# A hybrid encoder in float32: keys projected ahead of queries, the memory's parts ahead of both, and one recurrent block kept on chip

## The chip, the cores and the metric

The kernel runs on one core of a Trainium2 chip. The metric is the device time of one execution in microseconds (us). The core has TensorE (matmuls, PE in the profile; its weight loads are PEld), VectorE (DVE), ScalarE (ACT), GpSimd (POOL, which here mostly issues DMAs) and SyncE (SP, which issues the other DMAs). SBUF is the memory on chip, PSUM the accumulators of TensorE, DRAM the memory off chip.

## The reference

Two layers over 512 positions of width 1024. Each layer projects its input `h` with one large matrix into the inputs of five branches: dilated attention (A), a recurrence run in both directions (B), grouped attention with rotation (C), differential attention (D) and attention to a memory of 256 rows (M). Their gated outputs go through one product each, weighted by a gate that is computed from `h`, and then through an output product and a layer norm.

```python
h = layer_norm(x, ln_in_g, ln_in_b)
for l in range(DEPTH):
    p = jnp.einsum('bsd,dc->bsc', h, w_in[l])
    pa, pb, pc, pd, pm = split_last(p, mixer_sizes)
    o_a = mixer_dilated(pa, table_a)
    o_b = mixer_rwkv(pb, ...)
    o_c = mixer_axial_gqa(pc, ...)
    o_d = mixer_diff(pd, ..., table_d, l)
    o_m = mixer_memory(pm, mem, w_mem_kv[l])
    y = gated_merge(h, (o_a, o_b, o_c, o_d, o_m), w_branch[l], w_gate[l], b_gate[l])
    out = jnp.einsum('bsd,de->bse', y, w_out[l])
    h = layer_norm(alpha * h + out, ln_g[l], ln_b[l])
```

`gated_merge` is the sum over the branches of `sigmoid(h @ w_gate + b_gate) * (o @ w_branch)`. In attention, `o = softmax(q kᵀ / 8 + bias) v`, per head of 64 channels (in D the difference of two such softmaxes).

## The kernel before

**Numbers and products.** Everything is float32. A value that enters a product is split into a high part, rounded to TensorE's faster float32 form, and a low rest: ScalarE casts the high part, VectorE subtracts it. `gemm3_steps` (lines 145 to 152) then makes three matmuls per block of 128 rows. `hT` holds the layer's input this way for the whole layer.

**A projection** (`proj`, lines 161 to 163) makes one block of 128 output channels for all 512 positions: 24 matmuls into a PSUM tile `pg`, of which there are two. Its weights come in two halves of 256 KB: `load_w` loads each into a slot `wraw` (two slots on each of the channels "r" and "f") over SP's queue, `split_w` (lines 129 to 138) casts it on ScalarE to `whi` and subtracts on VectorE to `wlo`, two slots each. So the weights of a following projection are loaded and split while TensorE works on the current one. `proj_halves` makes two projections at once, in two stretches of 256 positions.

**Attention.** For a pair of heads (A, M) or one head of D the program projects the query, then the key, then the value. `q_stack` (lines 420 to 425) brings the query into high and low parts with two ScalarE and two VectorE instructions. `k_stack` (lines 427 to 437) does the same for the key, and then copies each of the four halves to the other 64 partitions by a DMA of 128 KB, issued on POOL's queue. `score` (lines 439 to 443) makes two matmuls for each block of 128 queries, one with `kh`, one with `kl`, into one of two PSUM tiles `psc`. `softmax` (lines 445 to 463) reads them on VectorE and ScalarE, `transposed` turns the result on TensorE, and `pv_head` or `pv` multiplies with the values. The value goes through the copy `vT` on ScalarE and four transposes on TensorE (line 501). `silu2` (lines 347 to 354) makes the gate, which takes one more projection, and `gated` multiplies it in, at the end of a pair or a head. In the first pair of A query and key are projected by `proj_halves`; in the first layer their weights are loaded at the kernel's start (line 285) and split at line 292.

**The memory.** In the first layer's first two pairs `memory_kv` (lines 260 to 266) projects the memory's keys and values for both layers and stores them in `scr_kv` in DRAM. Branch M (lines 681 to 702) loads them with one DMA of 512 KB into a tile `kvm` of a pool that is opened after D's pool is closed, projects the query, and then stacks the key and splits the value.

**Branch products.** The outputs of C, D and M, and of the recurrence's four blocks (pairs of heads, `finish`, lines 1054 to 1086), are stored in `scr_o` in DRAM (`spill`, and lines 1082 and 1085). `branch_steps` (lines 369 to 392) makes a branch's gate and product for eight blocks of channels; `reload` (lines 361 to 367) loads the outputs over POOL's queue into tiles `o`, of which there are four. The products of A, C, D and M are steps of the generator `fl`, from which `pull` takes some during C, M and the recurrence, so that TensorE has work between the steps of a slow chain. The product of the recurrence (line 1134) is made in the last stage of a layer together with the output product, the residual `z` and the layer norm.

**The order.** The program gives no order across engines. The framework plans it when the program is built: what comes earlier in the program has priority, instructions are placed as they become ready and as tile slots come free, and each engine and each DMA queue then works in that fixed order. In the trace, matmuls of a following projection stand between scores, for instance. A pool opened later may use the memory of a closed one only after the last use of its tiles.

Of the kernel before, what the change touches and what calls it, by code (L numbers as in the profile page):

```python
# [9 lines left out]
F32 = mybir.dt.float32  # L10
# [9 lines left out]
S = 512  # L20
# [32 lines left out]
def encoder_kernel(ctx: ExitStack, tc: tile.TileContext, x, mem, ln_in, rel_bias, w_in, par, w_up, a_up,  # L53
# [218 lines left out]
    with tc.tile_pool(name="init", bufs=1) as ip:  # L272
# [11 lines left out]
        load_x(3)  # L284
        raws = [load_w(w_in[0, b], 1024, ch) for b, ch in zip((0, 4), "rf")]
        for t in range(2):
# [37 lines left out]
    for l in range(L):  # L324
# [10 lines left out]
        ot = []  # L335
        y = [None] * 8

        def new_o():
# [29 lines left out]

        def branch_steps(br, os, nk, done=None, ch="f", pool=wp, gb=1):
            k0 = K0[br]  # L370
            if os is None:
                os = reload(br, nk)
            for db in range(8):
                ps = ps_f() if ch == "f" else ps_s()
                w = split_w(w_gate[l, br * 8 + db], 1024, "f")
                yield from gemm3_steps(ps, [(*wk(w, k), hT[:, 0, k, :], hT[:, 1, k, :]) for k in range(8)])
                gt = pool.tile([128, S], F32, name="gt", tag="gt", bufs=gb)
                i = br * 8 + db
                act(gt, ps, AF.Tanh, scale=0.5, bias=hb[:, i:i + 1])
                ps = ps_f() if ch == "f" else ps_g()  # L380
                w = split_w(w_branch[l, db, :, k0 * 128:(k0 + nk) * 128], nk * 128, ch)
                yield from gemm3_steps(ps, [(*wk(w, k), os[k][:, 0, :], os[k][:, 1, :]) for k in range(nk)])
                if y[db] is None:
                    y[db] = big.tile([128, S], F32, name="y", tag="y", bufs=8)
                    stt(y[db], gt, 1.0, ps, ALU.add, ALU.mult)  # L385
                else:
                    stt(gt, gt, 1.0, ps, ALU.add, ALU.mult)  # L387
                    if done is None:
                        tt(y[db], y[db], gt, ALU.add)
                    else:  # L390
                        tt(gt, y[db], gt, ALU.add)
                        done(db, gt)
# [17 lines left out]
        with tc.tile_pool(name=f"att{l}", bufs=1) as at:  # L410
# [115 lines left out]
            for hp in range(4):  # L526
# [5 lines left out]
                if hp == 0:  # L532
                    proj_halves((ps, ps2), l, (0, 4), hT, "rf", ws0 if l == 0 else None)
                else:
                    proj(ps, l, hp, hT)
                    proj(ps2, l, 4 + hp, hT, "f")
                q = q_stack(ps)
                k = k_stack(ps2)
                ps = ps_g()
# [4 lines left out]
                if l == 0 and hp < L:  # L544
                    for b in range(4):
                        memory_kv(hp, b)
                of = tile_of("of", [128, S], F32, 2)
                for i in range(2):
                    b = load_bias(2 * hp + i)
# [6 lines left out]
                    pv_head(of, p4, 4, lambda kb: v[:, i, kb, :], i)  # L556
                g2 = silu2(at, l, 12 + hp, ch="f")
                oA.append(gated(of, g2))
# [69 lines left out]


            with tc.tile_pool(name=f"attd{l}", bufs=1) as ad:  # L630
                lt = ad.tile([128, 4, 64], F32, name="lt", tag="lt")
# [11 lines left out]
                for h in range(4):  # L643
                    ps = ps_g()
                    proj(ps, l, 44 + h, hT)
                    q = q_stack(ps)
                    ps = ps_g()
                    proj(ps, l, 48 + h, hT)
                    k = k_stack(ps)
                    ps = ps_g()  # L650
# [29 lines left out]

            with tc.tile_pool(name=f"attm{l}", bufs=1) as am:
                kv = am.tile([128, 4, 256], F32, name="kvm", tag="kvm")
                nc.sync.dma_start(out=kv, in_=scr_kv[l].rearrange("b p t -> p b t"))
                for b in range(2):
                    ps = ps_g()
                    proj(ps, l, 60 + b, hT)
                    q = q_stack(ps)
                    k = k_stack(kv[:, b, :], 256)
                    v = v_pair(kv[:, 2 + b, :], 2)
                    of = tile_of("of", [128, S], F32, 2)  # L690
                    for i in range(2):
                        p4 = []
                        for qb in range(4):
                            ps = ps_s()
                            score(ps, q, k, i, qb, 256)
                            p, _ = softmax(ps, 256, None, (DVE, ACT)[qb % 2])
                            p4.append(p)
                            pull(0.3)
                        pv_head(of, p4, 2, lambda kb: v[:, i, kb, :], i)
                    g2 = silu2(at, l, 62 + b)  # L700
                    t = gated(of, g2, True)
                    spill(4, b, t)


        with tc.tile_pool(name=f"rw{l}", bufs=1) as rp:
# [6 lines left out]
            def recurrence():  # L712
# [341 lines left out]
                def finish(p):  # L1054
# [23 lines left out]
                    g2 = silu2(rp, l, 16 + 14 + p, 1, "ysq")  # L1078
                    stt(ys, ys, 0.5, g2, ALU.mult, ALU.mult)
                    hi = rp.tile([128, S], F32R, name="yhi", tag="ysq", bufs=1)  # L1080
                    nc.scalar.copy(hi, ys)
# [30 lines left out]
        with tc.tile_pool(name=f"out{l}", bufs=1) as op:  # L1112
# [20 lines left out]
            gb = load_gb(op, lnp[l])  # L1133
            for _ in branch_steps(1, None, 4, done, "r", op, 2):
                pass
# [137 lines left out]
```

## Time and profile before

| | us |
|---|---|
| median of 3 runs | 2314.18 |
| lowest and highest run | 2313.76, 2317.56 |
| profiled execution | 2311.92 |
| its span, first to last instruction | 2310.1 |
| TensorE busy | 2206.5 (96%) |
| VectorE busy | 1733.0 (75%) |
| ScalarE busy | 1273.5 (55%) |
| mean granted TensorE clock | 0.991 of full |

In the profiled execution the first layer's A runs to about 215 us, C to about 345, D to about 490, M to about 530, the recurrence to about 1056 and the layer's last stage to about 1180; the second layer follows with the same stages. The profile is read from TensorE: where a matmul is preceded by idle time, the view of waits names what released it. Times of the timeline count from the first instruction.

### The profile page before, as it was taken

Reading aid. Unit: us, or ns where it says so; the run is one execution under the profiler, and the core shown is the slowest. Engines: PE = TensorE matmul, PEld = TensorE weight load, DVE = VectorE, ACT = ScalarE, POOL = GpSimd, SP = SyncE. Lnnn points to the kernel's source line nnn. Section 1 sums busy time; section 2 is a strip of 40 time slices with the busy share of each in tenths; the row PEclk is TensorE's granted clock in tenths of the full one; section 3 lists DMA queues with packets and bytes.
Section 4 is the critical chain, followed back from the end, with each engine's and each line's share of the span. In section 5 each row is a group of like instructions: output and inputs, shape, how many; then the busy total and the mean of one; then the engine's idle time right before and its main releaser. Section 6 shows DMA issues by size and latency. Waiting matters only on the chain.

```text
span 2310.1 us, 36289 instructions
## 1 busy us (share of the span) xinstructions
PE 2206.5 (96%) x13056; PEld 1690.5 (73%) x13056; DVE 1733.0 (75%) x4236; ACT 1273.5 (55%) x2785; POOL 60.9 (3%) x119
## 2 busy tenths in 40 slices
PE   6999999999999999999999999999999999999998
PEld 5877777777677777776877777777677777777676
DVE  7676886576889797965567778766778979878455
ACT  3555666675655565544235656666675646555440
POOL 0000000000000000000000000000000000000000
PEclk9999999999999999999999999999999999999999
DMA  7733123332222221315334321232312222222350
GB/s 261 230 95 86 64 76 96 105 95 80 73 79 70 93 77 60 108 51 190 101 116 104 94 64 62 94 99 83 114 60 92 74 65 94 72 93 67 100 180 37
DMA packets 112612, 222.58 MB, mean 96 GB/s; under 512 B 13304, under 2 KB 23288, under 8 KB 112048
## 3 DMA queue, kind: packets, MB, share of 16 engines
q1 hardware_dynamic: 102000, 196.14, 26.5%
q0 software_dynamic: 10432, 24.12, 4.1%
q8 instruction: 103, 1.69, 0.3%
q14 instruction: 77, 0.63, 0.1%
HBM read 188.71 MB, written 28.36 MB: 94 GB/s over the span
## 4 chain that ended last, share of the span: by engine, by line
PE 53%; issue 17%; DVE 17%; ACT 7%; DMA 5%; POOL 0%; SPq 0%; DVEq 0%; POOLq 0%; ACTq 0%
PE pg L150 7%; PE pg L151 7%; PE pg L149 7%; PE pf L149 5%; PE pf L150 4%; PE pf L151 4%; PE psc L443 3%; DVE pr L959 2%; DVE W L961 2%; PE po L488 2%; PE pt L469 2%; DVE wlof L136 1%; PE psc L151 1%; PE psc L150 1%; PE psc L149 1%
## 5 line engine op out<-in xcount | busy, mean ns | idle before, releaser
L150 PE MATMUL pg<-hT,whir 128*128 128x512 f32 (+1 forms) x912 | 366.0, 401 | 0.5 <-DVE hT L176 0.5
L149 PE MATMUL pg<-hT,whir 128*128 128x512 f32 (+1 forms) x912 | 364.4, 400 | 1.9 <-DVE q L424 1.6
L151 PE MATMUL pg<-hT,wlor 128*128 128x512 f32 (+1 forms) x912 | 364.3, 399 | 1.7 <-DVE wlor L136 1.7
L136 DVE TENSOR_TENSOR wlor<-wrawr,whir 128x512 fp32r<-128x512 f32 x240 | 163.7, 687 | 123.2 <-ACT whir L135 114.5
L135 ACT CAST whif<-wrawf 128x512 fp32r<-128x512 f32 (+1 forms) x272 | 164.6, 606 | 149.9 <-PE pf L150 87.4
L135 ACT CAST whir<-wrawr 128x512 fp32r<-128x512 f32 x240 | 147.5, 618 | 178.4 <-PE pg L150 111.9
L149 PE MATMUL pf<-hT,whif 128*128 128x512 f32 x512 | 223.0, 435 | 8.9 <-DVE y L385 5.0
L136 DVE TENSOR_TENSOR wlof<-wrawf,whif 128x512 fp32r<-128x512 f32 (+1 forms) x272 | 181.6, 669 | 48.3 <-ACT whif L135 43.1
L150 PE MATMUL pf<-hT,whif 128*128 128x512 f32 x512 | 208.3, 407 | 0.0
L151 PE MATMUL pf<-hT,wlof 128*128 128x512 f32 x512 | 207.7, 406 | 0.0
L151 PEld LDWEIGHTS pg<-hT,wlor 128*128 128x128 f32 x912 | 172.2, 189 | 40.6 <-DVE wlor L136 4.2
L149 PEld LDWEIGHTS pg<-hT,whir 128*128 128x128 f32 x912 | 172.4, 189 | 38.8 <-ACT whir L135 2.6
L150 PEld LDWEIGHTS pg<-hT,whir 128*128 128x128 f32 x912 | 172.2, 189 | 37.8 <-issue 3.6
L176 DVE TENSOR_TENSOR pT<-pt,pT 128x512 fp32r<-128x512 f32 x176 | 114.2, 686 | 36.3 <-ACT pT L175 34.9
L175 ACT CAST pT<-pt 128x512 fp32r<-128x512 f32 x176 | 94.6, 588 | 63.7 <-PE pt L469 62.6
L149 PEld LDWEIGHTS pf<-hT,whif 128*128 128x128 f32 x512 | 97.5, 190 | 41.2 <-DVE gt L387 10.7
L469 PE MATMUL pt<-cst,p 128*128 128x128 f32 x704 | 118.6, 273 | 0.0
L151 PEld LDWEIGHTS pf<-hT,wlof 128*128 128x128 f32 x512 | 97.3, 190 | 22.4 <-issue 1.6
L959 DVE TENSOR_TENSOR pr<-W,U 128x60 f32<-128x60 f32 (+24 forms) x496 | 103.8, 209 | 11.9
L150 PEld LDWEIGHTS pf<-hT,whif 128*128 128x128 f32 x512 | 98.0, 191 | 18.9 <-issue 3.9
L961 DVE TENSOR_TENSOR W<-W,pr 128x60 f32<-128x60 f32 (+24 forms) x496 | 102.8, 207 | 10.8
L469 PEld LDWEIGHTS pt<-cst,p 128*128 128x128 f32 x704 | 89.7, 141 | 27.3 <-DVE p L460 2.9
(324 smaller groups left out, 4836.9 us busy)
## 6 DMA issues: line engine op xcount, KB each, us to landing
wrawr<-in_w_in_dram SPq DMA_DIRECT2D x224, 256.0 KB, 2.8
wrawf<-in_w_gate_dram SPq DMA_DIRECT2D x160, 256.0 KB, 2.8
o<-scr_o POOLq DMA_DIRECT2D x28, 512.0 KB, 4.5
wrawf<-in_w_branch_dram SPq DMA_DIRECT2D x48, 256.0 KB, 2.7
bias<-scr_toe SPq DMA_DIRECT2D x24, 448.0 KB, 3.3
scr_o<-os SPq DMA_DIRECT2D x20, 512.0 KB, 3.1
wrawf<-in_w_in_dram SPq DMA_DIRECT2D x32, 256.0 KB, 3.2
wrawr<-in_w_out_dram SPq DMA_DIRECT2D x32, 256.0 KB, 3.0
```

What stands on the lines that cost most here:

```text
L135: nc.scalar.copy(hi, raw)
L136: tt(lo, raw, f(hi), ALU.subtract)
L149: mm(ps, ah, bh, start=(i == 0), stop=False)
L150: mm(ps, ah, bl, start=False, stop=False)
L151: mm(ps, al, bh, start=False, stop=(i == n - 1))
L175: nc.scalar.copy(hi, src)
L176: tt(lo, src, f(hi), ALU.subtract)
L443: mm(ps[:, :nk], q[:, i, sl], part[:, i if g is None else g, :nk], start=(j == 0), stop=(j == 1))
L469: nc.tensor.transpose(pt[:, qb * 128:(qb + 1) * 128], p4[qb][:, kb * 128:(kb + 1) * 128], ident)
L488: mm(po, vwin(kb), pT[:, b, :], start=(kb == 0 and b == 0), stop=(kb == nkb - 1 and b == 1))
L959: tt(pr, W[:, t8, s:s + 1].to_broadcast([128, nt, n]), U[:, s:s + 1, rsl].to_broadcast([128, nt, n]), ALU.mult)
L961: tt(W[:, t8, rsl], W[:, t8, rsl], pr, ALU.add)
```

## The change

1. In A and D the key is projected and stacked ahead of the query. In the first pair of A, key and query change places in the interleaved projection; the key keeps channel "r" of the two. In the other pairs the key takes channel "r" and the query "f".
2. In the first pair of A the gate's projection (`silu2`) stands ahead of the scores instead of behind the products.
3. The memory's keys and values are loaded ahead of D, into the two tiles `qf` that C used, by two DMAs of 256 KB. In M the key is stacked and the value split ahead of the query's projection.
4. The recurrence's last block (p = 3) is split into a tile `o` and stays on chip: it is neither stored nor reloaded. The branch product of the recurrence starts with this block; `order` keeps weights and blocks together.

```diff
-        raws = [load_w(w_in[0, b], 1024, ch) for b, ch in zip((0, 4), "rf")]
+        raws = [load_w(w_in[0, b], 1024, ch) for b, ch in zip((4, 0), "rf")]
...
+        oB = []
...
-        def branch_steps(br, os, nk, done=None, ch="f", pool=wp, gb=1):
+        def branch_steps(br, os, nk, done=None, ch="f", pool=wp, gb=1, order=None):
...
-                yield from gemm3_steps(ps, [(*wk(w, k), os[k][:, 0, :], os[k][:, 1, :]) for k in range(nk)])
+                yield from gemm3_steps(ps, [(*wk(w, k), o[:, 0, :], o[:, 1, :]) for k, o in zip(order or range(nk), os)])
...
                 if hp == 0:
-                    proj_halves((ps, ps2), l, (0, 4), hT, "rf", ws0 if l == 0 else None)
+                    proj_halves((ps2, ps), l, (4, 0), hT, "rf", ws0 if l == 0 else None)
                 else:
-                    proj(ps, l, hp, hT)
-                    proj(ps2, l, 4 + hp, hT, "f")
+                    proj(ps2, l, 4 + hp, hT)
+                    proj(ps, l, hp, hT, "f")
+                k = k_stack(ps2)
                 q = q_stack(ps)
-                k = k_stack(ps2)
...
                 of = tile_of("of", [128, S], F32, 2)
+                g2 = silu2(at, l, 12 + hp, ch="f") if hp == 0 else None
                 for i in range(2):
...
-                g2 = silu2(at, l, 12 + hp, ch="f")
+                g2 = g2 or silu2(at, l, 12 + hp, ch="f")
...
+            kvm = [tile_of("qf", [128, S], F32, 2).rearrange("p (b t) -> p b t", b=2) for _ in range(2)]
+            for i in range(2):
+                nc.sync.dma_start(out=kvm[i], in_=scr_kv[l, 2 * i:2 * i + 2].rearrange("b p t -> p b t"))
...
                 for h in range(4):
                     ps = ps_g()
+                    proj(ps, l, 48 + h, hT)
+                    k = k_stack(ps)
+                    ps = ps_g()
                     proj(ps, l, 44 + h, hT)
                     q = q_stack(ps)
-                    ps = ps_g()
-                    proj(ps, l, 48 + h, hT)
-                    k = k_stack(ps)
...
-            with tc.tile_pool(name=f"attm{l}", bufs=1) as am:
-                kv = am.tile([128, 4, 256], F32, name="kvm", tag="kvm")
-                nc.sync.dma_start(out=kv, in_=scr_kv[l].rearrange("b p t -> p b t"))
-                for b in range(2):
-                    ps = ps_g()
-                    proj(ps, l, 60 + b, hT)
-                    q = q_stack(ps)
-                    k = k_stack(kv[:, b, :], 256)
-                    v = v_pair(kv[:, 2 + b, :], 2)
...
+            for b in range(2):
+                k = k_stack(kvm[0][:, b, :], 256)
+                v = v_pair(kvm[1][:, b, :], 2)
+                ps = ps_g()
+                proj(ps, l, 60 + b, hT)
+                q = q_stack(ps)
...
                     stt(ys, ys, 0.5, g2, ALU.mult, ALU.mult)
+                    if p == 3:
+                        oB.append(finish_o(rp, ys))
+                        return
                     hi = rp.tile([128, S], F32R, name="yhi", tag="ysq", bufs=1)
...
-            for _ in branch_steps(1, None, 4, done, "r", op, 2):
+            for _ in branch_steps(1, oB + reload(1, 3), 4, done, "r", op, 2, (3, 0, 1, 2)):
```

The rest of branch M is the same text, one level further out.

## Rows read from the trace of the kernel before

**Rows 1.** The page: busy time of each engine, share of the span, instructions.

```profile
PE 2206.5 (96%) x13056; PEld 1690.5 (73%) x13056; DVE 1733.0 (75%) x4236; ACT 1273.5 (55%) x2785; POOL 60.9 (3%) x119
```

**Rows 2.** Whom TensorE waited for, whole span: us in total, times, longest us.

```profile
PE psc L443 <- DMA kl<-kl: 9.0, 9, 3.1
PE pg L149 <- DMA o<-scr_o: 8.4, 2, 5.2
PE psc L443 <- DMA kh<-kh: 6.1, 12, 1.0
PE pt L501 <- DMA kvm<-scr_kv: 1.4, 2, 0.8
```

**Rows 3.** Stretches: length, busy us (instructions) per engine; then TensorE clock, DMA share, GB/s.

```profile
386.78:393.00 6.22, 6.13 (x21) 4.80 (x22) 4.71 (x15) 4.03 (x10) 0.00 (x0) 0.73 0.15 43
1069.29:1075.00 5.71, 5.71 (x18) 4.54 (x19) 2.34 (x4) 2.20 (x5) 0.00 (x0) 0.70 0.82 310
1198.20:1204.00 5.80, 5.80 (x20) 4.64 (x21) 5.37 (x18) 3.65 (x10) 0.00 (x0) 0.71 0.19 57
1512.33:1519.00 6.67, 6.23 (x20) 4.59 (x21) 4.43 (x12) 4.02 (x9) 0.00 (x0) 0.74 0.16 49
2197.56:2205.00 7.44, 7.44 (x22) 5.87 (x23) 3.77 (x6) 2.75 (x5) 0.00 (x0) 0.64 0.30 115
```

**Rows 4.** Whom TensorE waited for in branch D: first layer, then second layer.

```profile
PE psc L443 <- DMA kh<-kh: 2.2, 4, 1.0
PE psc L443 <- DMA kl<-kl: 1.5, 2, 1.2
...
PE psc L443 <- DMA kl<-kl: 3.9, 4, 2.2
PE psc L443 <- DMA kh<-kh: 2.5, 4, 1.0
```

**Rows 5.** One projection of 24 matmuls as a stretch, in the columns of rows 3.

```profile
1189.10:1194.74 5.64, 5.64 (x24) 4.59 (x25) 2.64 (x4) 1.47 (x3) 2.07 (x4) 1.00 0.89 252
```

**Rows 6.** Timeline, one head of D: start, us, engine, instruction, [idle before]; then loads' landing.

```profile
1506.02 0.33 SPq L359 DMA_DIRECT2D scr_o<-os  x1
1508.35 0.51 POOL L436 DMA_DIRECT2D kl<-kl  x1 [0.22 <-issue]
1512.33 0.50 PE L443 MATMUL psc<-kl,q 128*128 128x512 f32 x1 [2.15 <-DMA kl<-kl]
1513.36 0.62 ACT L135 CAST whir<-wrawr 128x512 fp32r<-128x512 f32 x1 [5.39 <-DMA wrawr<-in_w_in_dram]
1514.01 0.59 ACT L653 COPY vT<-pg 128x512 f32<-128x512 f32 x1
...
DMA to landing us min/median/max: 2.7/2.9/5.9
```

**Rows 7.** Timeline, second layer, first head pair of A.

```profile
1198.20 0.47 PE L443 MATMUL psc<-kl,q 128*128 128x512 f32 x1 [3.06 <-DMA kl<-kl]
1198.40 0.29 DVE L635 TENSOR_TENSOR lp<-lt 128x128 f32<-128x128 f32 x1 [5.08 <-DMA lt<-in_d_lambda_dram]
```

**Rows 8.** The first layer: last reader of tile qf, and (timeline) first use of kvm.

```profile
L424 DVE SCALAR_TENSOR_TENSOR q<-qf,q x2: 685/686/687, 306.7 to 307.5; 64x512 fp32r<-64x512 f32 x2
...
495.19 0.41 PE L501 MATMUL pt<-cst,kvm 128*128 128x128 f32 x2 [0.59 <-DMA kvm<-scr_kv]
```

**Rows 9.** Timeline, end of the second layer's recurrence; then its stall as a stretch.

```profile
2184.40 0.68 DVE L1084 TENSOR_TENSOR ys<-ys,yhi 128x512 fp32r<-128x512 f32 x1
2185.11 0.36 SPq L1085 DMA_DIRECT2D scr_o<-ys  x1
2189.34 0.54 POOL L365 DMA_DIRECT2D o<-scr_o  x1 [6.04 <-DMA scr_o<-ys]
2197.56 0.79 PE L149 MATMUL pg<-o,whir 128*128 128x512 f32 x1 [5.18 <-DMA o<-scr_o]
...
2192.00:2197.60 5.60, 0.42 (x3) 0.04 (x1) 0.03 (x1) 0.00 (x0) 0.00 (x0) 0.86 1.04 385
```

More of the change, by code (lines that the diff above doesn't have):

```diff
@@ L678, in encoder_kernel @@
                     spill(3, h, t)
-            with tc.tile_pool(name=f"attm{l}", bufs=1) as am:
-                kv = am.tile([128, 4, 256], F32, name="kvm", tag="kvm")
-                nc.sync.dma_start(out=kv, in_=scr_kv[l].rearrange("b p t -> p b t"))
-                for b in range(2):
-                    ps = ps_g()
-                    proj(ps, l, 60 + b, hT)
-                    q = q_stack(ps)
-                    k = k_stack(kv[:, b, :], 256)
-                    v = v_pair(kv[:, 2 + b, :], 2)
[L690 to L702, printed above, removed]
+            for b in range(2):
[4 more added lines that the diff above has]
+                q = q_stack(ps)
+                of = tile_of("of", [128, S], F32, 2)
+                for i in range(2):
+                    p4 = []
+                    for qb in range(4):
+                        ps = ps_s()
+                        score(ps, q, k, i, qb, 256)
+                        p, _ = softmax(ps, 256, None, (DVE, ACT)[qb % 2])
+                        p4.append(p)
+                        pull(0.3)
+                    pv_head(of, p4, 2, lambda kb: v[:, i, kb, :], i)
+                g2 = silu2(at, l, 62 + b)
+                t = gated(of, g2, True)
+                spill(4, b, t)
         with tc.tile_pool(name=f"rw{l}", bufs=1) as rp:
```

## The prediction

> **What bounds the kernel now.** I read the page's busy times first: TensorE is busy 96% of the span, VectorE 75%, ScalarE 55% [rows 1]. So time comes back only where TensorE stands still and the work behind the stall isn't held by something else at the same moment. The list of who TensorE waited for shows which stalls the change can reach [rows 2]: the score matmuls (line 443) wait for the copies of the key halves, 9.0 us for `kl` and 6.1 us for `kh`; the first branch product after the recurrence waits 8.4 us in two places for the reload of `o` from DRAM; the transposes of the memory's values wait 1.4 us for `kvm`. Together 24.9 us of 2310.1.
>
> Then I read the granted clock in the stretches right behind the five longest of these stalls [rows 3]. It is a mean of stretches at the upper and at the lower level (2.4 and 1.2 GHz): 0.73, 0.70, 0.71, 0.74 and 0.64. TensorE is busy in nearly all of them, so each costs (1 − clock) × its length: 1.7, 1.7, 1.7, 1.7 and 2.7 us, in sum 9.5. A stall of 2 to 5 us is thus followed here by another 1.7 to 2.7 us lost to slow matmuls. The ceiling of the change is 24.9 + 9.5 = 34.4 us.
>
> By stage: the differential branch (D) has waits of 2.2 + 1.5 us in the first layer and 3.9 + 2.5 in the second [rows 4], 10.1, and two of the slow stretches (behind 386.78 and 1512.33), 13.5 together. The dilated branch (A) has the rest of the 15.1, 5.0, of which 3.1 is one stall (the longest for `kl` [rows 2]) in the second layer's first head pair, and the slow stretch behind 1198.20: 6.7. The end of the recurrence has 8.4 + 1.7 + 2.7 = 12.8. Memory has 1.4.
>
> **Keys ahead of queries, branch D.** No instruction is added or removed; a projection (24 matmuls in 5.64 us at full clock [rows 5], 0.235 us each), its two casts, two subtractions and four half copies on the POOL queue change places with the query's projection, two casts and two subtractions. Today the copies are issued at the end of the value projection: in the worst head the last goes out at 1508.35, and TensorE, which stopped at 1510.18 after the first score, goes on at 1512.33 [rows 6]. One projection earlier, the copies have 5.6 us more, above the longest wait of 3.1 us, so the wait itself goes. What is late next shows in the same head: ScalarE's next weight cast starts at 1513.36, after 5.39 us of waiting for a DMA; the value copy `vT` is queued behind it, at 1514.01, and four transposes on TensorE behind that. The weight transfer took up to 5.9 us where the median of this stretch is 2.9 [rows 6], since it shares its time with the four key copies and with the spill issued at 1506.02 [rows 6]. With the copies gone and the spill still there I take 3.5 us, nearer to the median because four of the five transfers in the way leave. The load that took 5.9 landed about 1513.3, so it was issued about 1507.4 and would land at 1510.9; `vT` follows 0.65 + 0.59 us later, at 1512.1. TensorE has three scores and one projection matmul until then, 4 × 0.235 us from 1510.18, that is to 1511.1: 1.0 us of the 2.5 stays in this head. Over the eight heads of both layers I charge 4.0 us, keeping 9.5 of 13.5. Bounds: nothing kept, if the load still takes 5.9; all, if it takes 2.9.
>
> The trace first, a rule beside it: the weight load issued on SP took twice its median while copies issued on POOL were in flight [rows 6]. The Trainium skill, "DMA: Bandwidth & Descriptors", section "Issuing engines are not separate DMA queues", says that transfers from the sync, scalar and gpsimd engines run on the same 16 DMA engines and interleave whoever started them. By that rule the copies, moved, slow the loads of the next projection instead; if the queues were separate, D would give its full 13.5, the charge below would be nothing, and the sum would be 30.7 in place of 24.0. The trace agrees with the rule.
>
> The copies now fall beside the loads for the query and value projections, in 16 places (4 pairs and 4 heads, two layers). The spill, which belongs to the head before, then lies elsewhere than the copies, so each load meets one of the two, not both. Bounds per place: nothing, to the 3.0 us by which the worst load exceeded its median plus 1.7 of slow clock. I charge 0.17 per place, 2.7 us in all, close to the lower end, because half of the loads of that stretch landed within 2.9 us [rows 6] and each is asked for before the projection that needs it.
>
> **Branch A.** In the second layer's first pair, scores wait 3.06 us for `kl` [rows 7]. Keys first brings their columns forward in the interleaved first projection, and the gate projection now put ahead of the scores gives TensorE 5.64 us of work exactly there. VectorE's first softmax step is meanwhile queued behind a small product for lambda that waits 5.08 us for its DMA until 1198.40 [rows 7]; today this is hidden behind the `kl` wait, and afterwards behind the gate projection. The price: that projection no longer fills gaps between softmax steps. The next pair's three projections do, so I charge 0.7 us and keep 6.0 of 6.7; bounds 1.1 kept (all 5.6 us come back as gaps) and 6.7.
>
> The same hoist and the swapped first loads sit in the first layer's opening, where the weight of one more projection is asked for before the first bias. One projection late or early is 5.64 us [rows 5]; I take zero, the middle, as TensorE has the memory's products to go on with there; bounds 5.6 either way.
>
> **Memory's parts.** The load of `kvm` (one 512 KB transfer on SP, now two of 256) waits no longer for a pool that opens after D, but for the two `qf` slots, whose last reader in the first layer starts at 307.5; its first use is at 495.19 [rows 8], so 180 us of other work hide it. It passes on SP the lambda load, the biases and the weight loads of D; had it to wait for a slot there, the weight loads behind it would wait too. Keys and values come ahead of the query projection: the 1.4 us go. Bounds 0 and 1.4.
>
> **The last recurrent block on chip.** Per layer this removes two stores of 256 KB on SP and one reload of 512 KB on POOL; cast and subtraction stay, into another tile. Today: the subtraction starts at 2184.40, the store goes out at 2185.11, the reload at 2189.34, when the store has landed, and TensorE stands 5.18 us until 2197.56 [rows 9]. Afterwards the block is ready at 2184.40 + 0.68 = 2185.1. The wait is 5.2 in one layer and 8.4 − 5.2 = 3.2 in the other; with the clock 12.8. Next late: the product starts with block 3, so products with blocks 0 and 1 that filled gaps earlier now follow 2185.1; a reload whose slot is freed at the end of the memory branch; and the weights for the next products, since the DMA engines were 1.04 busy in the stall [rows 9], though 1 MB less is now asked of them. I charge 1.5 us a layer and keep 9.8. Bounds: 0 (these loads were hidden by the stall and are all as late as it) and 12.8.
>
> **Sum.** 9.5 + 6.0 + 1.4 + 9.8 − 2.7 = 24.0 us. The profiled execution took 2311.92 (span 2310.1 and 1.8 around it): 2287.9. The median of the runs, 2314.18, lies 2.3 above it, so I forecast 2290.
>
> **Rivals.** (1) The copies and loads only trade places: each D head stalls on `vT` as long as it stalled on the keys. For it: casts and copies became ready within 1.1 us of each other in the head shown [rows 6]; against it: of the five transfers in the way only the spill stays. D's 9.5 are lost: 2300. The rule of the Trainium skill named above would make it so. (2) The end of the recurrence waits for weights instead of the reload: for it the busy DMA engines; against it 1 MB less. Alone it gives 24.0 − 9.8 = 14.2, again 2300; with (1), 24.0 − 9.5 − 9.8 = 4.7 are left: 2309. (3) Slower: the moved copies delay the second half of a running projection's weights, in mid-projection where TensorE has nothing else. A place costs 3.0 + 1.7 = 4.7 us; gains without the charge are 26.7, so it decides from six of the 16 places; at eight it is 37.6 − 26.7 = 10.9 slower, 2325. Against it: half of the loads land within 2.9 us even where copies and spill meet [rows 6]. (4) The order of instructions is planned anew by the framework; if the plan puts queries and scores where they were, only crumbs are left: 2314.
>
> **How the numbers follow.** Forecast 0.62, (1) or (2) alone 0.17, both 0.08, (3) 0.06, (4) 0.07. The forecast's own range runs from 2280 (the ceiling; 2278 with some of the opening's 5.6) to 2297; with (1) and (2) to 2309. A change of 0.2%, 4.6 us, is about what a measurement here can tell from none. Faster 0.87, same 0.07, slower 0.06.
>
> **What would show it.** Right: no line-443 wait on `kh` or `kl` over 0.5 us, none on `o<-scr_o` in the last stage, full clock behind 385, 1198, 1512 and the ends of both recurrences. D's step is wrong if line 501 waits for `vT` over 1 us per head; the tail if the first products wait for `whif` or `whir` over 2 us; the moved copies if matmuls of lines 149 to 151 wait for `whir` in mid-projection; the hoist if TensorE has gaps between the first pair's softmax steps. A wrong total with right steps would mean stalls in places untouched, by the new plan.

## The result and the profile after

The median of the changed kernel is 2259.62 us (4 runs, 2257.58 to 2261.37) against 2315.87 before (4 runs, 2313.76 to 2317.68): a ratio of 0.9757, 95% interval 0.974 to 0.9774. That is 56 us less where 24 were forecast, and below the low end of the range. The profiled execution took 2261.37 us with a span of 2259.6, so 50.5 us of span are to be found.

The page of the changed kernel, busy time of each engine as in [rows 1]:

```profile
PE 2186.5 (97%) x13056; PEld 1678.6 (74%) x13056; DVE 1730.6 (77%) x4236; ACT 1273.2 (56%) x2785; POOL 59.6 (3%) x117
```

TensorE makes the same 13056 matmuls in 20.0 us less busy time, and its idle time fell by 30.5. The busy time is mostly the clock: summed over windows of one microsecond, busy time × (1 − granted clock) was 17.9 us before and is 0.0 now. No stretch at the lower level is left in which TensorE works.

Whom TensorE waited for in the changed kernel, whole span (us in total, times, longest), the largest rows after the first weights' load; it answers [rows 2], and many lines of the kernel have moved by one to seven:

```profile
PE pt L1035 <- DVE PE L1027: 7.0, 10, 0.9
PE pf L149 <- ACT gt L380: 5.0, 12, 0.7
PE pm L149 <- ACT whif L135: 3.6, 2, 2.2
PE psc L149 <- ACT whif L135: 3.0, 4, 1.0
PE pf L149 <- DVE gt L388: 2.8, 8, 0.7
PE pt L502 <- ACT vT L660: 2.8, 5, 1.2
PE pg L151 <- DVE wlor L136: 2.1, 5, 1.2
PE pt L981 <- DVE U L977: 1.9, 4, 0.8
```

All four rows of [rows 2] are gone. But two more rows, which the prediction doesn't name, went or shrank: the one for `y` is gone, the one for `U` fell from 5.3 to 1.9 us. In the same view of the kernel before they read:

```profile
PE pt L977 <- DVE U L973: 5.3, 4, 1.9
PE pf L149 <- DVE y L385: 5.0, 2, 2.5
```

Where the time went shows in the stores of `scr_o`, one at the end of each head or block. Timeline of SP in the first layer, the kernel before: the last stores of D and M, the first of the recurrence.

```profile
489.18 1.28 SPq L359 DMA_DIRECT2D scr_o<-os  x1
531.01 0.33 SPq L359 DMA_DIRECT2D scr_o<-os  x1
715.51 0.33 SPq L1082 DMA_DIRECT2D scr_o<-yhi  x1
```

The same three in the changed kernel:

```profile
483.77 0.33 SPq L360 DMA_DIRECT2D scr_o<-os  x1
520.01 0.33 SPq L360 DMA_DIRECT2D scr_o<-os  x1
699.72 0.33 SPq L1089 DMA_DIRECT2D scr_o<-yhi  x1
```

M, from store to store, went from 41.83 to 36.24 us, and the start of the recurrence from 184.50 to 179.71, though no line of the recurrence's start was changed. Differences of such stores give the whole table (first layer + second; "alone" is the experiment with this part only; A is the stretch from the last transpose of the layer's input to C's first store; the last stages run from the third block's store to the next layer's A, or to the end):

| stage | forecast | whole change | part alone |
|---|---|---|---|
| D | 9.5 | 5.7 + 7.8 = 13.5 | 7.6 + 8.8 = 16.4 |
| moved copies, in A and D | −2.7 | in these rows | |
| A, second layer | 6.0 | 7.1 | 7.1 |
| M | 1.4 | 5.6 + 5.9 = 11.5 | 5.6 + 5.9 = 11.5 |
| start of the recurrence | 0 | 4.8 + 3.6 = 8.4 | 4.9 + 3.5 = 8.3 |
| last stages of both layers | 9.8 | 4.0 + 6.9 = 10.9 | 4.6 + 7.4 = 12.0 |
| all else | 0 | −0.9 | |
| sum | 24.0 | 50.5 | |

### The profile page after: what moved, and what is told of

Read it like the earlier page. It is cut to its first block, busy times and chain, and to the rows that moved or that the text cites. A ratio compares the mean times of both kernels' runs of the same rounds, so it can differ in the third digit from the quotient of the medians.

```text
span 2259.6 us, 36239 instructions
## 1 busy us (share of the span) xinstructions
PE 2186.5 (97%) x13056; PEld 1678.6 (74%) x13056; DVE 1730.6 (77%) x4236; ACT 1273.2 (56%) x2785; POOL 59.6 (3%) x117
## 4 chain that ended last, share of the span: by engine, by line
PE 70%; DVE 14%; ACT 8%; DMA 5%; issue 3%; DVEq 0%; POOL 0%; ACTq 0%; SPq 0%
PE pg L150 10%; PE pg L151 10%; PE pg L149 10%; PE pf L149 6%; PE pf L150 5%; PE pf L151 5%; PE psc L444 4%; PE po L489 3%; PE pt L470 3%; DVE W L965 2%; DVE pr L963 2%; DMA wrawr<-in_w_out_dram 1%; DVE wlof L136 1%; PE po L479 1%; DMA wrawf<-in_w_mem_dram 1%
## 5 line engine op out<-in xcount | busy, mean ns | idle before, releaser
L149 PEld LDWEIGHTS pf<-hT,whif 128*128 128x128 f32 x512 | 96.5, 188 | 35.8 <-DVE gt L388 10.2
```

Of the source, the lines that this page charges most:

```text
L149: mm(ps, ah, bh, start=(i == 0), stop=False)
```

## The experiments

The theory to test: the memory part carries about 20 us, by way of M and the start of the recurrence behind it. The rival: each part gives only the waits that it removes, and the surplus comes from parts acting together.

### Each part alone

**Memory part** (the load before D into the query tiles, key and value ahead of the query in M):

```diff
+            kvm = [tile_of("qf", [128, S], F32, 2).rearrange("p (b t) -> p b t", b=2) for _ in range(2)]
+            for i in range(2):
+                nc.sync.dma_start(out=kvm[i], in_=scr_kv[l, 2 * i:2 * i + 2].rearrange("b p t -> p b t"))
...
+                    k = k_stack(kvm[0][:, b, :], 256)
+                    v = v_pair(kvm[1][:, b, :], 2)
                     ps = ps_g()
                     proj(ps, l, 60 + b, hT)
                     q = q_stack(ps)
-                    k = k_stack(kv[:, b, :], 256)
-                    v = v_pair(kv[:, 2 + b, :], 2)
```

> Only the memory's parts are moved ahead (load into the query tiles before D, key and value ahead of the query's projection); D, A and the end of the recurrence as before. Theory 1 (the surplus of the whole change comes from here): the span between D's last spill and M's last spill, 41.8 and 42.2 us before and 36.2 and 36.3 with the whole change, falls to 36 to 37 in both layers; the wait of 2.5 us for y disappears; with the calmer start of the recurrence (184.5 us from M's last spill to the first block's store, 179.7 with the whole change) the total falls by about 20 us, to about 2296. Theory 2 (a part gives no more than the waits it removes and the slow clock behind them; the surplus comes from parts acting together): by 1 to 2 us, to about 2314, and M still takes 41 us or more.

Measured: 2296.54 us against 2313.93, ratio 0.9925 (0.9912 to 0.9938), 17.4 us less. M took 36.24 and 36.26 us, the start of the recurrence 179.65 and 180.02; the wait for `y` is gone. Theory 1 holds: these stages come out within 0.2 us of the whole change. Of the total, 17.4 us came where about 20 were expected.

**Keys ahead of queries in D:**

```diff
                     ps = ps_g()
+                    proj(ps, l, 48 + h, hT)
+                    k = k_stack(ps)
+                    ps = ps_g()
                     proj(ps, l, 44 + h, hT)
                     q = q_stack(ps)
-                    ps = ps_g()
-                    proj(ps, l, 48 + h, hT)
-                    k = k_stack(ps)
```

> Only in D the key is projected ahead of the query. Theory 1 (the waits and the slow clock behind them go in full, nothing is late next): 13.5 us less, about 2302, and no matmul of line 501 waits over 1 us. The forecast's reading: 9.5 less what the moved copies cost (1.4 of the 2.7 for D's eight places), about 8 us less, 2308. Rival 1 of the prediction: copies and weight loads trade places, no more than 2 us less, 2314, with line 501 waiting for vT over 1 us in each head.

Measured: 2293.63, ratio 0.9914 (0.9898 to 0.9929), 20.3 less. By the stores D took 16.4 less; the last stages, which this edit doesn't touch, happened to be 4.7 us shorter in the same execution. Whom TensorE waited for in D, first layer, then (behind the "...") second, in place of [rows 4]:

```profile
PE pg L151 <- DVE wlor L136: 0.3, 1, 0.3
PE pt L501 <- ACT vT L653: 0.3, 1, 0.3
...
PE pt L501 <- ACT vT L653: 0.9, 1, 0.9
PE pg L151 <- DVE wlor L136: 0.3, 1, 0.3
```

`vT` is late by 1.2 us in eight heads, not by the 4.0 that were charged. The landing of the copies points to the reason. DMA issues in the first layer's D (KB each, median us from issue to landing), kernel before:

```profile
wrawr<-in_w_in_dram SPq DMA_DIRECT2D x32, 256.0 KB, 3.0
kh<-kh POOLq DMA_DIRECT2D x8, 128.0 KB, 4.2
kl<-kl POOLq DMA_DIRECT2D x8, 128.0 KB, 4.3
```

and with D's keys first:

```profile
wrawr<-in_w_in_dram SPq DMA_DIRECT2D x33, 256.0 KB, 2.8
kh<-kh POOLq DMA_DIRECT2D x6, 128.0 KB, 3.1
kl<-kl POOLq DMA_DIRECT2D x6, 128.0 KB, 3.1
```

Both sides got faster: the copies, issued ahead of the spill instead of right behind it, land in 3.1 us (median), and the longest weight load fell from 5.1 to 4.3 us (second layer 5.9 to 3.9).

**Branch A** (key and query change places; the first pair's gate ahead of the scores):

```diff
-                    proj_halves((ps, ps2), l, (0, 4), hT, "rf", ws0 if l == 0 else None)
+                    proj_halves((ps2, ps), l, (4, 0), hT, "rf", ws0 if l == 0 else None)
...
+                g2 = silu2(at, l, 12 + hp, ch="f") if hp == 0 else None
                 for i in range(2):
...
-                g2 = silu2(at, l, 12 + hp, ch="f")
+                g2 = g2 or silu2(at, l, 12 + hp, ch="f")
```

> Only A: key and query change places and the first pair's gate projection stands ahead of the scores. By the forecast 6.0 us less, about 2310, all of it in the second layer's first pair, the first layer within 1 us. If the hoisted projection is missed later as filler: 1 us less, 2315. If the parts only work together, no change.

Measured: 2303.4, ratio 0.9957 (0.9943 to 0.997), 10.5 less. The second layer's A went from 211.96 to 204.85 us, 7.1 less, of which 4.7 are idle time and 1.7 slow clock. The first layer up to C's end took 341.5 us against 343.3; that stretch varies between 341.5 and 344.6 over the runs here, so nothing follows from it.

**The last block on chip** (the block kept, and the product's order):

```diff
+                    if p == 3:
+                        oB.append(finish_o(rp, ys))
+                        return
...
-            for _ in branch_steps(1, None, 4, done, "r", op, 2):
+            for _ in branch_steps(1, oB + reload(1, 3), 4, done, "r", op, 2, (3, 0, 1, 2)):
```

> Only the last recurrent block stays on chip and its product starts with it. Theory 1 (all of the stall goes and its slow clock with it): 12 to 13 us less, about 2303. The forecast's reading: 9.8 less, about 2306. Rival 2 of the prediction (weights are late next): no more than 2 us less, 2314, and the first products of the last stage wait for their weight halves over 2 us.

Measured: 2302.01, ratio 0.9945 (0.9929 to 0.9961), 11.9 less, 12.0 by the stores of the last stages. No matmul waits for `o` any more; the last stages begin with waits of 0.5 and 1.3 us for a weight's cast.

The four gains make 60.1 us against the 56 of the whole change (each is known to some 3 us): the surplus is in the parts, not between them. That leaves why the memory part is worth 17, not 1.4.

### What in the memory part does it

**The early load without the new order** (query's projection first again):

```diff
                     ps = ps_g()
                     proj(ps, l, 60 + b, hT)
                     q = q_stack(ps)
-                    k = k_stack(kv[:, b, :], 256)
-                    v = v_pair(kv[:, 2 + b, :], 2)
+                    k = k_stack(kvm[0][:, b, :], 256)
+                    v = v_pair(kvm[1][:, b, :], 2)
```

> Of the memory's two edits only the early load (into the query tiles, before D); the query's projection still stands ahead of key and value. Theory 1 (before, the load waits for D's end, M's first scores come late, TensorE spends the projections that it could do meanwhile, and has none at M's end): nearly the whole gain of the memory part stays, M at 36 to 38 us in both layers and 15 to 19 us less in all, about 2297. Theory 2 (the order of key, value and query makes it): no more than the 1.4 us of the wait, M at 40 us or more.

Measured: 2292.52, ratio 0.9913 (0.9889 to 0.9937); M 35.48 in both layers, the recurrence's start 181.24 and 181.13.

**The new order without the early load:**

```diff
+                    k = k_stack(kv[:, b, :], 256)
+                    v = v_pair(kv[:, 2 + b, :], 2)
                     ps = ps_g()
                     proj(ps, l, 60 + b, hT)
                     q = q_stack(ps)
-                    k = k_stack(kv[:, b, :], 256)
-                    v = v_pair(kv[:, 2 + b, :], 2)
```

> Of the memory's two edits only the order: key and value ahead of the query's projection, the load as before (one transfer into a pool that opens after D). Theory 1 (the late load is the cause): M stays at 41 to 43 us, the total within 4 us of the kernel before. Theory 2 (the order is the cause): M at 36 to 38 us, 15 to 19 us less.

Measured: 2312.07, ratio 0.9997 (0.9984 to 1.0009); M 42.12 and 41.82. The load makes all of it; the order is worth nothing.

**The pool kept.** With the early load the pool `attm` is gone, and the recurrence's tiles could lie elsewhere or come free earlier. Here it is opened again:

```diff
+            with tc.tile_pool(name=f"attm{l}", bufs=1) as am:
...
+                pad = am.tile([128, 4, 256], F32, name="pad", tag="pad")
+                nc.gpsimd.memset(pad, 0.0)
```

> The whole memory part as in the first experiment, but the pool that the old load used is still opened after D and holds an unused tile of its size, filled once, so that the recurrence's pool opens behind it and lies as before. If the 8.3 us at the recurrence's start (4.8 and 3.5 between M's last spill and the first block's store) come from M's earlier end and fuller supply of projections: they stay, 17 to 19 us less in all. If they come from the pool that is gone (where the recurrence's tiles lie and when they are free): they go, 10 to 12 us less, with M at 36 us all the same.

Measured: 2294.41, ratio 0.9925 (0.9901 to 0.9949); M 36.24 and 36.25, the recurrence's start 179.59 and 179.97. The pool plays no part.

**The transfer itself.** M's own data early, and the old transfer at M's start as well, read by nobody:

```diff
+                pad = am.tile([128, 4, 256], F32, name="pad", tag="pad")
+                nc.sync.dma_start(out=pad, in_=scr_kv[l].rearrange("b p t -> p b t"))
```

> The whole memory part as in the first experiment (M's own data come early), and in addition the old transfer of 512 KB at M's start, into a tile that nothing reads. If before the change the late data cost M its time: M stays at 36 to 37 us, 17 to 20 us less in all than before. If the transfer cost it, by holding back the weight loads beside it: M at 40 us or more and at most 10 us less in all.

Measured: 2296.3, ratio 0.9922 (0.9905 to 0.9939); M 36.26 and 36.25. Not the 512 KB beside the weights cost the time, but that M's data came late.

**Later still.** The kernel before, with its load issued twice:

```diff
                 nc.sync.dma_start(out=kv, in_=scr_kv[l].rearrange("b p t -> p b t"))
+                nc.sync.dma_start(out=kv, in_=scr_kv[l].rearrange("b p t -> p b t"))
```

> The kernel before, with M's load issued twice into the same tile, the second after the first, so that keys and values are some 4 to 6 us later still (a transfer took 4.7 us from issue to first use). If lateness at M's start is paid at M's end, because the projections that cover it are used up: M grows by 3 to 6 us in each layer to 45 to 48, its direct wait for kvm stays under 2 us, and the total is 6 to 12 us longer, 2320 to 2326. If the scheduler's cover takes it all (lateness isn't paid): M within 1 us and the total within 4 us of before.

Measured: 2315.98 against 2313.21, ratio 1.0011 (1.0001 to 1.0021). In the first layer `kvm` is first used 9.9 us behind D's last store instead of 6.0, and M takes 46.00 us instead of 41.83 (second layer 45.57, 3.4 more), as the theory said. But the total grew by 2.8 us, not by 6 to 12. Whom TensorE waited for in that M:

```profile
PE pf L149 <- DVE y L385: 1.1, 1, 1.1
PE pt L501 <- DMA kvm<-scr_kv: 0.7, 1, 0.7
PE psc L443 <- DMA kh<-kh: 0.4, 1, 0.4
```

The wait that bears the load's name is as short as before (0.7 against 0.6), and the one for `y` is shorter (1.1 against 2.5). M is longer because more work stands in it. The first layer's M as a stretch, TensorE alone (length, busy us (matmuls), clock, DMA share, GB/s), in the kernel before and in this one:

```profile
489.18:531.01 41.83, 38.19 (x192) 0.99 0.37 114
...
491.66:537.66 46.00, 43.24 (x212) 1.00 0.39 126
```

The 20 matmuls more are branch products (tile `pf`), of which the recurrence's start has 20 fewer. TensorE's idle time in M and the recurrence's start of both layers together is 24.5 us against 24.4. So this lateness was covered by work of the stage that follows, and M's length is not what it cost. What it left is a new stall in the recurrence's start (for `AR`, 2.8 and 2.7 us) and 16.0 us of slow clock there, where the kernel before lost 8.5 in one execution and 10.2 in another.

### Beside the other parts, and again

**The whole change without the memory part.** From the changed kernel:

```diff
-            kvm = [tile_of("qf", [128, S], F32, 2).rearrange("p (b t) -> p b t", b=2) for _ in range(2)]
...
+            with tc.tile_pool(name=f"attm{l}", bufs=1) as am:
+                kv = am.tile([128, 4, 256], F32, name="kvm", tag="kvm")
+                nc.sync.dma_start(out=kv, in_=scr_kv[l].rearrange("b p t -> p b t"))
```

> The whole change without the memory part. If the parts add up: 2259.6 plus what the memory part is worth alone, 17 to 19 us, so 2276 to 2279, with M at 42 us and a wait of 2.5 us for y in each layer. If the memory part gains only beside the others or they beside it: under 2268 or over 2286.

Measured: 2271.6, ratio 0.9826 (0.981 to 0.9842). So in company the memory part is worth 12.0 us by the two medians (2271.6 − 2259.6), or 14.6 if each is taken against the kernel before as measured beside it (41.6 and 56.2 less), where 17 to 19 were expected. M still took 42.04 and 41.47 us, but the recurrence's start only 180.98 and 182.68. Its idle time there was as before (8.7 and 9.5 us against 8.2 and 8.6); what was missing was the slow clock. Three of its stretches, each from the end of a stall for `y` or `U` on, which are 2.5 and 1.9 us long as in the kernel before (columns of [rows 3]):

```profile
523.27:530.50 7.23, 5.85 (x24) 4.44 (x24) 3.91 (x12) 2.79 (x6) 1.28 (x3) 1.00 0.52 186
620.51:630.00 9.49, 9.43 (x139) 7.02 (x140) 7.77 (x23) 5.50 (x14) 0.00 (x0) 1.00 0.18 57
1723.76:1733.00 9.24, 9.18 (x137) 6.78 (x138) 7.57 (x22) 5.30 (x13) 0.00 (x0) 1.00 0.19 61
```

**The same kernel, profiled a second time:**

> The whole change without the memory part, profiled a second time. The first profile lost 0 and 1.7 us to a lower clock at the recurrence's start, with the same stalls as the kernel before (idle 8.7 and 9.5 us). If the loss belongs to this kernel's order of work: 0 and 1.7 again. If it depends on the moment: other multiples of 1.7 in at least one layer, at the same idle time.

Measured: 2274.98 us. The stretches behind the same three stalls now:

```profile
521.74:529.00 7.26, 7.26 (x24) 5.60 (x24) 3.05 (x11) 1.58 (x3) 1.31 (x3) 0.76 0.41 150
619.72:629.00 9.28, 9.28 (x87) 6.85 (x87) 5.79 (x14) 4.20 (x11) 0.00 (x0) 0.63 0.19 57
1725.18:1734.00 8.82, 8.82 (x86) 6.78 (x87) 5.79 (x14) 4.08 (x11) 0.00 (x0) 0.63 0.21 62
```

The loss at the recurrence's start is 4.9 and 5.1 us where it was 0 and 1.7, with the same instructions and nearly the same idle time (8.4 and 8.2). Whether such a stall is followed by the lower clock depends on the execution, and with it what the memory part is worth: 2274.98 − 2258.57 = 16.4 us between these second profiles of this kernel and of the changed one.

**The kernel before, a second time:**

> The kernel before, unchanged, profiled a second time. Between M's last spill and the first recurrent block's store the first profile lost 4.8 and 3.4 us to a lower granted clock behind stalls of 1.9 to 2.5 us. If the lower clock belongs to the stall: 4.8 and 3.4 again, within 0.5. If it depends on the moment: other multiples of 1.7 us, from 0 to 5.1, at the same idle time of 8.2 to 8.7 us.

Measured: 2316.66 us; losses of 5.1 and 4.6 at the start of the recurrence (4.8 and 3.4 in the first profile), 22.7 us in the whole span (17.9). Only part of it repeats.

**The changed kernel, a second time:**

> The changed kernel, profiled a second time. If it has no stall left that is followed by a lower clock: no loss in any stage again, and its time within 3 us of 2259.6. If its full clock was chance: at least 1.7 us of loss, behind one of its stalls of 0.9 to 2.2 us.

Measured: 2258.57 us, and 0.0 us lost to the clock again. Its stalls behind the opening are all under 1.3 us, and none of them was followed by the lower level in either execution. The opening holds longer ones, the longest behind the first weights a wait for a weight's cast (2.2 us in the first execution, 1.8 in the second), and the full clock followed it both times. In the second profile of the kernel without the memory part the lower level followed the same wait. The stretches behind it, the changed kernel first (behind 2.2 us), then that profile (behind 2.3 us), in the columns of [rows 3]:

```profile
53.75:60.00 6.25, 6.21 (x39) 4.95 (x39) 5.52 (x15) 4.38 (x11) 0.00 (x0) 1.00 0.76 235
...
53.64:60.00 6.36, 6.36 (x32) 5.57 (x33) 4.33 (x12) 4.05 (x10) 0.00 (x0) 0.73 0.68 231
```

So the 0.0 is in part luck.

### Two more

**Only the gate's projection ahead of the scores in A's first pair:**

```diff
+                g2 = silu2(at, l, 12 + hp, ch="f") if hp == 0 else None
                 for i in range(2):
...
-                g2 = silu2(at, l, 12 + hp, ch="f")
+                g2 = g2 or silu2(at, l, 12 + hp, ch="f")
```

> Of A's two edits only the first pair's gate projection ahead of the scores; query before key as before. If the projection as cover for the key copies makes A's gain (10.5 us with both): 7 us or more less. If the key's place makes it: 3 us or less, and the first pair of the second layer still waits over 1 us for a key half.

Measured: 2306.57, ratio 0.9973 (0.9962 to 0.9984), 7.1 less; the second layer's A took 206.16 us, 5.8 of the 7.1 gained with both edits. The projection as cover makes most of A's gain; 1.3 us are left for the key's place.

**The changed kernel with the value ahead of the query in D:**

```diff
+                    proj(ps, l, 52 + h, hT)
+                    vT = tile_of("vT", [128, S], F32, 1)
+                    nc.scalar.copy(vT, ps)
+                    v = v_parts(vT, 4)
+                    ps = ps_g()
                     proj(ps, l, 44 + h, hT)
                     q = q_stack(ps)
```

(the same four lines behind the query are taken out)

> The changed kernel with one more move in D: the value is projected between key and query, so that its copy and transposes come ahead of the scores. If the waits for vT that are left in D (2.8 us in all) are reachable: 2 to 4 us less than the changed kernel, 2256. If the query's two casts and subtractions are then late for the scores in the same way: within 2 us of the changed kernel's 2259.6, with score matmuls waiting for q.

Measured: 2261.59, ratio 0.9779 (0.9764 to 0.9793): no better than the change. D itself became 3 us longer in each layer (143.19), M 3 us shorter (32.9), and the recurrence's start 2 us longer (181.8 and 181.6), with a new stall of 2.0 us and 1.7 us of slow clock behind it in each. In the first layer's D the waits for `vT` fell from 1.4 to 0.5 us, but a score then waited 1.1 us for a softmax (0.4 before), and TensorE's idle time stayed at 2.6 us. No score waited for the query.

## Why the prediction was right and wrong

**Wrong: "Keys and values come ahead of the query projection: the 1.4 us go. Bounds 0 and 1.4."** This term measured 19.9 us in M and the start of the recurrence, and it is 18.5 of the 26.5 us by which the sum was short. It took the price of late data from the wait that bears their name. In the kernel before, the order of work was planned round the late load. M's first score stood 9.0 us behind D's last store (498.2 against 489.18); in the changed kernel it stands 4.1 us ahead of it (479.68). TensorE filled that time with projections, and lacked them at M's end. TensorE's time on projections (tile `pg`) in four quarters of M, the kernel before:

```profile
489.18:499.64 10.46, 9.47 (x40) 1.00 0.69 206
499.64:510.10 10.46, 6.45 (x21) 1.00 0.27 72
510.10:520.55 10.45, 6.67 (x22) 1.00 0.33 116
520.55:531.01 10.46, 5.38 (x17) 0.97 0.19 62
```

and in the changed kernel:

```profile
483.77:492.83 9.06, 5.81 (x20) 1.00 0.43 147
492.83:501.89 9.06, 6.84 (x28) 1.00 0.18 58
501.89:510.95 9.06, 6.65 (x22) 1.00 0.36 118
510.95:520.01 9.06, 8.38 (x33) 1.00 0.26 81
```

Forty projection matmuls stand in M's first quarter and 17 in its last; now it is 20 and 33. So in the kernel before the chain at M's end (softmax, transposes, product, gate) lay bare, and TensorE stood 2.52 us until VectorE had added the last product into `y`, a step queued behind that chain's own. Timeline of the kernel before (by engine, not every line):

```profile
528.37 0.68 DVE L495 TENSOR_TENSOR of<-of,g 128x512 f32<-128x512 f32 x1
529.09 0.69 DVE L385 SCALAR_TENSOR_TENSOR y<-gt,pf 128x512 f32<-128x512 f32 x1
529.83 0.50 PE L149 MATMUL pf<-hT,whif 128*128 128x512 f32 x1 [2.52 <-DVE y L385]
```

The row for `y` stood in the same list as the 1.4 us, with 5.0 us, unused. The idle time of M and the recurrence's start together fell from 24.4 us to 9.8, and the loss to the clock from 8.5 to 0. That the early load is the cause is shown (load alone, order alone, pool kept, transfer added). How it shortens the stalls is read from these rows and not shown by itself, and the run with the load later still warns against too simple a reading: there M's last quarter had no projection at all, and yet the idle time did not grow, since branch products stood in. How the fuller supply shortens the stalls inside the recurrence's start, for example the one for `U` from 1.9 us to 0.2, was not taken apart further.

**Wrong by the same mistake: "The ceiling of the change is 24.9 + 9.5 = 34.4 us."** It held only waits with the names of the edited tiles, and only the slow stretches behind them. The loss to the clock was 17.9 us in that execution; 8.5 of it lay at M's end and the start of the recurrence. The sum of all was 50.5: idle 30.5, clock 17.9, and 2.1 that the busy time hides, probably because the last matmul before a stop is shown 0.39 us long where in a stream the next one starts after 0.235. One reading was off without consequence: the slow stretch behind 386.78 follows two stalls of 1.2 and 1.0 us [rows 4], not one of 2 to 5.

**Right in kind, too cautious: D.** The waits went in full. The 4.0 us for `vT` and the 2.7 for the moved copies were not to be paid: with keys first alone D came out at 16.4 us, in the whole change at 13.5. The difference of 2.9 is idle time (5.1 us in D against 2.0), nearly all in D's last head, in which M's work now starts (36.3 and 35.5 us long, 34.3 and 34.5 with D's edit alone). Of rival (1), that copies and loads only trade places, nothing is left. The rule that it leaned on (the Trainium skill, "DMA: Bandwidth & Descriptors", section "Issuing engines are not separate DMA queues": transfers run on the same 16 DMA engines whoever issues them) agrees with the copies' 4.2 us right behind the spill and 3.1 ahead of it. The four copies of a head are now also issued over 3.3 to 4.7 us instead of 2.1, and no run separates the two. What did not follow is a loss: the weight loads of the first layer's D got no slower (2.8 us in the median against 3.0). That D gave 16.4 where the prediction counted 13.5 at most lies in the busy time again: idle time fell by 9.5 us and the loss to the clock by 3.3, and the rest, 3.6, is time that TensorE was shown busy with the same matmuls. Nor is the gain exact: in six executions with D and the memory's load as before (two of them of the kernel before itself) D took 293.7 to 298.4 us in both layers together, and the profile that the prediction read, 293.9, was at the short end.

**Right: A (6.0 forecast, 7.1) and the last stages (9.8 forecast, 10.9; 12.0 alone).** The charges of 0.7 and of 1.5 per layer were small enough. That the last stages came so near is partly luck: where no edit touched them, they took 417.4 to 422.9 us in both layers together, and 422.1 in the profile that the forecast read. Rival (2) fell: the last stages' first matmuls wait 1.0 us for a weight's cast, not over 2. The opening stayed as it was.

**The rest of the miss:** the forecast put the median 2.3 us above the profiled execution; the median before was 4.0 above it, and the median after 1.8 below its own.

**Rivals (3) and (4)** did not happen: no matmul stands in mid-projection for over 1.2 us, and the plan did move the instructions.

## What to carry to other kernels

When independent work fills the time until late data arrive, the wait that bears the data's name doesn't tell what the lateness costs: ask where that work will be missing, and look at the end of the stage and the start of the next for stalls under other names. Price such an edit by the idle time and slow clock from the stage's start to the next stage that runs full, not by the stage's length: a stage can grow because it takes in work of the next one. And set a ceiling from all the stalls of the stages that an edit touches, not from the rows that it names.

## What the runs showed of the hardware

The same stall is not always followed by a lower clock. Behind stalls of 1.9 to 2.5 us at the same places, with the same instructions (the kernel without the memory part, twice), the granted clock was 1.00, 1.00 and 1.00 in one execution and 0.76, 0.63 and 0.63 in the next, a mean of stretches at 2.4 and 1.2 GHz. In two executions each of that kernel and of the kernel before, the losses at the recurrence's start were 0, 1.7, 3.4 and 4.6 to 5.1 us, near multiples of 1.7. The Trainium skill, "TensorE: Matmul & The Clock Gate", section "Part 1: The HAM clock gate (the "warmup" mystery)", says that the gate's clockwork runs free and isn't set by the kernel's start, so that the moment at which it changes differs between runs. It says this of a kernel's first matmuls; these two executions agree with it for drops in the middle of a kernel, without showing the clockwork itself. So a sum over one profile's slow stretches is one draw: for the kernel before, two executions lost 17.9 and 22.7 us. The changed kernel lost 0.0 twice. It has fewer such stalls, but the one in its opening was followed by the lower level in other executions, so its 0.0 need not repeat.
